# Moving seven fp32 load issues from ScalarE to SyncE, and pairing VectorE's result copies, in a batched 64x64 matmul

## Chip, cores, metric

One core of a Trainium2 chip. The metric is the device time of one execution in microseconds (us). The kernel before takes 135.17 us (median of 3 runs, 135.17 to 135.28), and its profiled execution has a span of 133.2 us.

## The reference

```python
a = randn(1024, 64, 64) fp32;  b = randn(1024, 64, 64) fp32
out = np.matmul(a, b)          # 1024 independent 64x64x64 products, fp32
```

The reference reads 33.55 MB and writes 16.78 MB.

## The kernel before

It walks 16 tiles of b and of the result (64 products each, 1 MB) and 8 tiles of a (128 products each, 2 MB). Three quarters of each a tile are loaded by GpSimd with a cast to bf16; the fourth comes as fp32 (`a_raw`) and is cast by VectorE. TensorE transposes a, VectorE spreads it into block-diagonal form (`at_bd`), TensorE multiplies, ScalarE and VectorE copy PSUM to `o_sb`, and GpSimd stores `o_sb` one tile later.

```python
A_AHEAD = 3; B_AHEAD = 4; HOLD = 2
o_v = out.rearrange("(t gh x) (mo w) n -> t (x mo) gh (w n)", gh=8, x=8, w=4)  # runs of 1 KB
# pools: a 3 buffers, b 4, work 2, o_sb 8 (1 MB each)
def load_a(s):
    ...                                       # h = 0..2: nc.gpsimd, fp32 -> bf16
    nc.scalar.dma_start(out=a_raw[...], in_=a_v[s, 3])                    # L72
def load_b(t):
    queue = nc.scalar if t % 2 else nc.sync                               # L91
    queue.dma_start(out=b_sb[:], in_=b_v[t])
def multiply(t):
    def put(lo, n):
        nc.gpsimd.dma_start(out=o_v[t, :, lo:lo+n, :], in_=o_sb[...])     # L161
    ...
    for half in range(2):
        ...                                   # 32 matmuls into o_ps, then 4 copies (L172)
        if not last:
            copies = [nc.scalar.copy] * 4
            if half:
                copies[3] = nc.vector.tensor_copy
            evacuate(o_ps, 4 * half, 4, copies)
    # stores: whole tiles; tile 14 in halves, tile 15 in quarters
...
for t in range(n_t):
    # spread and cast of t+1, load_b(t + B_AHEAD), on even t load_a(t//2 + 1 + A_AHEAD),
    # multiply(t), regroup / transpose of the next a, store(t-1)
```

## Time and profile before

| | before |
|---|---|
| time | 135.17 us (135.17 to 135.28) |
| span of the profiled run | 133.2 us |
| TensorE / VectorE / ScalarE / GpSimd busy | 51 / 72 / 65 / 27 % of the span |
| bytes at the memory | 33.55 MB read, 16.78 MB written |
| last load landed / last store issued / last store landed | 113.70 / 128.45 / 131.74 us |

Busy shares say little here: they average stages with different limits. Two views disagree about what bounds the kernel: the strip of slices shows the DMA engines full almost from end to end, and the chain that ended last is mostly compute:

```profile
DVE 29%; ACT 18%; PE 15%; DMA 13%; issue 10%; ACTq 7%; POOL 3%; SPq 1%; POOLq 1%; DVEq 0%
```

ACTq is ScalarE's own queue of issues; 7% of the chain is time in which ScalarE was held by an issue.

### The profile page before, as it was taken

What the parts mean: (1) busy time and instruction counts of PE and PEld (TensorE: products, weight loads), DVE (VectorE), ACT (ScalarE), POOL (GpSimd) and SP (SyncE); (2) the same over time, 40 slices, a digit from 0 to 9 for tenths busy, and PEclk for the clock granted to TensorE, in tenths of its full rate; (3) what the DMA queues carried; (4) which work ended last, traced back from release to release, by engine and by line L of the source; (5) the groups of instructions that cost most, each with busy time, mean ns of one, the idle gap of its engine ahead of it and who ended that gap; (6) DMA issues with size and microseconds to landing.
All of it is one profiled execution on the core that took longest, in us unless ns stands there. A gap on an engine that the chain in (4) does not pass through costs nothing.

```text
span 133.2 us, 2835 instructions
## 1 busy us (share of the span) xinstructions
PE 67.9 (51%) x1152; PEld 62.6 (47%) x1152; DVE 96.3 (72%) x121; ACT 86.8 (65%) x160; POOL 35.9 (27%) x49
## 2 busy tenths in 40 slices
PE   0000900784539259486358637951996195269300
PEld 0000900784439257475257527941995094268200
DVE  5920064943999249996999899799969996897740
ACT  3105525089950699489939992998399759969910
POOL 8981004000802017112413302030203020322460
PEclk9999995589965865579977985698569959955955
DMA  3999999999999999999999999999999999999893
GB/s 75 365 335 310 308 308 328 318 304 306 314 328 341 389 321 318 336 400 386 367 307 294 394 404 387 323 302 335 399 394 396 387 397 402 400 404 388 298 320 133
DMA packets 17485, 45.01 MB, mean 338 GB/s; under 512 B 1088, under 2 KB 1088, under 8 KB 17472
## 3 DMA queue, kind: packets, MB, share of 16 engines
q0 software_dynamic: 7440, 22.28, 54.7%
q10 hardware_dynamic: 5520, 13.11, 25.6%
q1 hardware_dynamic: 4512, 9.44, 20.1%
q8 instruction: 9, 0.15, 0.4%
q14 instruction: 4, 0.03, 0.1%
HBM read 33.55 MB, written 16.78 MB: 378 GB/s over the span
## 4 chain that ended last, share of the span: by engine, by line
DVE 29%; ACT 18%; PE 15%; DMA 13%; issue 10%; ACTq 7%; POOL 3%; SPq 1%; POOLq 1%; DVEq 0%
ACT o_sb L172 16%; DVE at_bd L128 14%; PE o_ps L184 13%; DMA b_sb<-in_b_dram 13%; DVE b_bf L139 6%; ACTq L72 4%; DVE o_sb L172 4%; POOL out_dram L161 3%; ACTq L91 3%; DVE a_bf L106 3%; PE at_ps L115 2%; DVE a_bf L103 2%; ACT b_bf L139 1%; SPq L85 1%; POOLq L274 1%
## 5 line engine op out<-in xcount | busy, mean ns | idle before, releaser
L172 ACT COPY o_sb<-o_ps 64x512 f32<-64x512 f32 x105 | 60.9, 580 | 20.3 <-PE o_ps L184 13.1
L184 PEld LDWEIGHTS <-at_bd 128*128 128x128 bf16 x1024 | 43.9, 115 | 35.5 <-DVE b_bf L139 25.1
L184 PE MATMUL o_ps<-b_bf,at_bd 128*128 128x64 bf16 x960 | 43.7, 218 | 31.2 <-DVE b_bf L139 22.4
L128 DVE COPY at_bd<-at_sb 32x1024 f32<-32x1024 f32 x64 | 45.6, 713 | 9.5 <-ACT at_sb L118 7.7
L161 POOL DMA_DIRECT2D out_dram<-o_sb x20 | 19.4, 968 | 77.9 <-DVE o_sb L172 72.5
L115 PE MATMUL at_ps<-identity,a_bf 128*128 128x128 f32 x128 | 23.3, 344 | 25.0 <-ACT a_bf L100 13.3
L115 PEld LDWEIGHTS at_ps<-identity,a_bf 128*128 128x128 f32 x128 | 19.3, 181 | 26.1 <-issue 20.8
L118 ACT COPY at_sb<-at_ps 128x512 f32<-128x512 f32 x32 | 17.4, 588 | 7.7 <-PE at_ps L115 7.3
L172 DVE COPY o_sb<-o_ps 64x512 f32<-64x512 f32 x15 | 10.4, 695 | 15.4 <-ACT o_sb L172 15.2
L139 DVE CAST b_bf<-b_sb 128x2048 bf16<-128x2048 f32 x14 | 17.4, 1245 | 0.4
L68 POOL DMA_DIRECT2D a_sb<-in_a_dram x21 | 12.5, 609 | 14.7 <-DVE a_bf L103 9.5
L106 DVE CAST a_bf<-a_raw 128x1024 bf16<-128x1024 f32 x7 | 7.0, 1003 | 1.9 <-DMA a_raw<-in_a_dram 1.9
L103 DVE COPY a_bf<-a_sb 128x3072 bf16<-128x3072 bf16 x7 | 6.7, 960 | 0.2
L100 ACT CAST a_bf<-o_sb 128x1024 bf16<-128x1024 f32 x2 | 2.0, 1042 | 7.4 <-issue 7.4
L100 DVE CAST a_bf<-o_sb 128x1024 bf16<-128x1024 f32 x2 | 2.5, 1228 | 2.6 <-DMA o_sb<-in_a_dram 2.6
L212 DVE MEMSET at_bd<- 128x4096 f32 x1 | 3.5, 3472 | 0.8 <-issue 0.8
L172 DVE COPY o_sb<-at_ps 64x256 f32<-64x256 f32 x8 | 3.4, 422 | 0.1
L139 ACT CAST b_bf<-b_sb 128x2048 bf16<-128x2048 f32 x1 | 1.9, 1898 | 2.3 <-DMA b_sb<-in_b_dram 2.3
L172 ACT COPY o_sb<-at_ps 64x256 f32<-64x256 f32 x8 | 2.9, 366 | 0.1
L209 ACT ACT_TABLE_LOAD x1 | 1.3, 1283 | 2.3 <-issue 2.3
L184 PE MATMUL at_ps<-b_bf,at_bd 128*128 128x64 bf16 x64 | 2.6, 212 | 0.3 <-DVE at_bd L128 0.3
L216 POOL MEMSET at_bd<- 128x2048 f32 x1 | 1.9, 1851 | 0.0
(12 smaller groups left out, 5.3 us busy)
## 6 DMA issues: line engine op xcount, KB each, us to landing
out_dram<-o_sb POOLq DMA_DIRECT2D x14, 1024.0 KB, 21.4
a_sb<-in_a_dram POOLq DMA_DIRECT2D x21, 256.0 KB, 19.7
a_raw<-in_a_dram ACTq DMA_DIRECT2D x7, 512.0 KB, 16.5
o_sb<-in_a_dram ACTq DMA_DIRECT2D x2, 512.0 KB, 7.3
o_sb<-in_a_dram SPq DMA_DIRECT2D x2, 512.0 KB, 6.4
out_dram<-o_sb POOLq DMA_DIRECT2D x2, 512.0 KB, 4.8
out_dram<-o_sb POOLq DMA_DIRECT2D x4, 256.0 KB, 3.7
b_sb<-in_b_dram SPq DMA_DIRECT2D x8, 0.5 KB, 16.8
```

The source lines that it names most:

```text
L68: nc.gpsimd.dma_start(out=a_sb[:, h, :, :].rearrange("p v k -> p (v k)"), in_=a_v[s, h])
L72: nc.scalar.dma_start(out=a_raw[:].rearrange("p v k -> p (v k)"), in_=a_v[s, 3])
L100: copy(a_bf[:, :, h, :], a_sb[h].rearrange("p (v k) -> p v k", v=16))
L103: nc.vector.tensor_copy(a_bf[:, :, 0:3, :], cast_sb[:].rearrange("p h v k -> p v h k"))
L106: nc.vector.tensor_copy(a_bf[:, :, 3, :], raw[:])
L115: nc.tensor.transpose(at_ps[:, vo, :], a_cols[:, 4 * vo + 2 * j + wl, :], identity[:])
L118: nc.scalar.copy(at_tiles[s][:, j, :, wl, :, :], at_ps[:].rearrange("p vo (g mp) -> p g mp vo", mp=4),)
L128: nc.vector.tensor_copy(bd[rows, :, :, :, h, :].rearrange("p j g wl mo -> p j (g wl) mo"), at_tiles[t // 2][rows, :, half, :, :, :].rearrange(
L139: (nc.vector.tensor_copy if t else nc.scalar.copy)(b_bf[:], b_sb[:])
L161: nc.gpsimd.dma_start(out=o_v[t, :, lo : lo + n, :], in_=o_sb[:, lo : lo + n].rearrange("p gh j wl n -> p (gh j wl n)"),)
L172: copies[2 * par + wl](dst, src)
L184: nc.tensor.matmul(o_ps[:, gl, g % 2, j, :], at_bd[:, j, g, :, u], b_bf[:, g, 64 * u : 64 * u + 64], start=(u == 0), stop=(u == 1),)
```

## The change

The intent is to take the slow issues of `a_raw` off ScalarE, which has copies to do, and give them to SyncE, which issues half of the b loads and does no arithmetic. VectorE's result copies, one per tile, become two on every odd tile, so that on even tiles VectorE does not wait for ScalarE. The first loads are reordered to suit SyncE's queue.

```diff
-        nc.scalar.dma_start(out=a_raw[:].rearrange("p v k -> p (v k)"), in_=a_v[s, 3])
+        nc.sync.dma_start(out=a_raw[:].rearrange("p v k -> p (v k)"), in_=a_v[s, 3])
@@ multiply
-                if half:
-                    copies[3] = nc.vector.tensor_copy
+                if half and t % 2:
+                    copies[2:] = [nc.vector.tensor_copy] * 2
@@ prologue
-        for t in range(3):
-            load_b(t)
+        load_b(0)
+        load_b(1)
         ...
         load_a(1)
+        load_b(2)
         nc.gpsimd.memset(bd_tiles[1][:, 1], 0.0)
-        for s in range(2, A_AHEAD):
-            load_a(s)
+        load_a(2)
```

## The prediction

> **What bounds the kernel now.** I read first the page's strip of forty slices and its byte counts, because the kernel does little arithmetic per byte.
>
> ```profile
> DMA  3999999999999999999999999999999999999893
> GB/s 75 365 335 310 308 308 328 318 304 306 314 328 341 389 321 318 336 400 386 367 307 294 394 404 387 323 302 335 399 394 396 387 397 402 400 404 388 298 320 133
> ...
> HBM read 33.55 MB, written 16.78 MB: 378 GB/s over the span
> ```
>
> The DMA row is full from the second slice to the last but two. The GB/s row seems to leave room (300 to 400), but a casting load counts only the bytes it writes: it reads 4 bytes for each 2 counted. The third line counts at the memory: 50.33 MB. I asked for busy time by stage next (columns after the length: busy time and count of PE, PEld, DVE, ACT and POOL, then granted clock, DMA share, GB/s).
>
> ```profile
> 0.00:10.00 10.00, 0.00 (x0) 0.00 (x0) 5.72 (x4) 1.48 (x3) 8.80 (x16) 1.00 0.80 258
> ...
> 70.00:80.00 10.00, 5.86 (x106) 5.18 (x103) 8.97 (x12) 9.79 (x19) 2.43 (x2) 0.84 1.05 364
> ...
> 110.00:120.00 10.00, 4.95 (x111) 4.50 (x110) 8.29 (x11) 8.65 (x16) 2.16 (x2) 0.81 1.03 402
> 120.00:133.00 13.00, 4.07 (x91) 3.79 (x88) 6.40 (x14) 6.75 (x15) 4.37 (x6) 0.63 0.80 287
> ```
>
> From 10 to 120 us the DMA share is above 1. No casting load is in flight after 94 us, so the 402 GB/s of 110 to 120 us is the rate at the memory. Counting each casting packet of the trace twice gives 405 GB/s for 5 to 20 us, 402 for 20 to 40, 400 for 40 to 60, and 394 to 396 from 60 to 113. The rate hardly moves while the engines go from nearly idle to busy, so I take about 400 GB/s as what the 16 DMA engines deliver here. Moving 50.33 MB at 402 takes 125.2 us of a span of 133.2.
>
> The chain of work that ended last tells another story, DVE 29% and ACT 18%, and the change is aimed at that one. The timeline shows a cause (columns: start, length, engine, line).
>
> ```profile
> 3.53 6.96 ACTq L72 DMA_DIRECT2D a_raw<-in_a_dram  x1
> ...
> 19.84 7.16 ACTq L72 DMA_DIRECT2D a_raw<-in_a_dram  x1
> ...
> 36.09 8.20 ACTq L72 DMA_DIRECT2D a_raw<-in_a_dram  x1
> ...
> 44.33 2.95 ACT L172 COPY o_sb<-o_ps 64x512 f32<-64x512 f32 x5 [5.95 <-PE at_ps L115]
> ...
> 86.69 0.69 DVE L172 COPY o_sb<-o_ps 64x512 f32<-64x512 f32 x1 [1.05 <-ACT o_sb L172]
> ```
>
> Issuing an fp32 a quarter occupies ScalarE's queue for up to 8.20 us; the copies behind it start only when it ends. The two others are 3.46 us at 53.27 and 4.22 at 65.23. Their ends (10.49, 27.00, 44.29, 56.73, 69.45) lie about half a microsecond after the landing of a transfer queued earlier on the same engine (9.99, 26.55, 43.65, 56.33, 68.97). So it is queue back-pressure: an issue that follows a b load waits until the work ahead of that b has drained.
>
> **What the Trainium skill says.** "DMA: Bandwidth & Descriptors", section "Issuing engines are not separate DMA queues", says that transfers issued by scalar, sync or gpsimd run on the same 16 DMA engines and that several issuers save only sequencer time. The trace agrees: three queues are active and their sum is pinned near 400 GB/s. "Perfetto Trace Analysis", section "Roofline", puts a single active core's practical ceiling at about 120% of 358 GB/s, about 430; the trace stays at 394 to 405, so I use the measured figure. The same page, section "DMA Instruction — HWDGE (DVE, Sync)", says the shown length of an issue includes waiting for the descriptor generator and generating; that fits issues of 0.54 to 8.20 us for equal transfers. It also calls that generator shared. The trace speaks against one engine's stalled issue holding up the other's: SyncE's b issue at 38.94 took 0.69 us inside ScalarE's 8.20 us stall. So moving the stalls to SyncE should not leave them on ScalarE.
>
> **The change part by part.** (1) Seven a-quarter issues leave ScalarE. They held its queue for 6.96 + 0.63 + 7.16 + 0.54 + 8.20 + 3.46 + 4.22 = 31.2 us, mostly while ScalarE had nothing to do. What lay on the chain: at 36.09 us. The interval between the waited-for DVE copies, 32.18, 48.49, 61.33, 73.88, 86.69, 99.51, 112.33, is 16.31 for the first pair of b tiles and 12.55 to 12.84 for the others, so that stall cost 3.5 us. At 19.84 it kept the at_sb copy until 27.05 although the first of its transposes, started at 24.15, was ready about 1 us later: 1 to 2 us. At 3.53 it kept the first a cast until 11.21, but the next things needed, b tile 0 (landed 19.81) and a quarter 1 (landed 23.28), are transfers, so nothing. Estimate for ScalarE: about 5 us off the compute chain.
>
> (2) VectorE's copies of result blocks: one per tile, 15 of 695 ns, become two on odd tiles and none on even ones, 14 in place of 15. ScalarE does 8 and 6 in place of 7 and 7. Sums hardly move. But the even tile's VectorE copy waited 1.05 us for ScalarE's third copy of the same half; that copy is now ScalarE's. Off VectorE before the even tile's a casts: 1.05 + 0.69 = 1.74 us. ScalarE's eighth copy delays its at_sb copies by 0.59: they would end near 101.15 where 100.57 was, and VectorE, ready at 100.35 in place of 102.09, would wait 0.8. The odd tile's two copies wait for the sixth ScalarE copy in place of the seventh. I make that pair 11.9 in place of 12.8: 0.9 a pair, over six steady pairs 5.4 us.
>
> (3) SyncE's order becomes b0, a1, b2, a2, a3, b4, a4, b6 and so on, with 13.1 MB on that queue and 9.4 on the other; before it was the other way round. a quarter 2 now follows b2. Before, it landed at 26.55 and b2 at 30.82. With a quarter 1 landing near 23.3, b2's 1.05 MB at about 105 GB/s to 33.3 and 0.52 MB at about 160 to 36.6, the a cast that ran at 33.78 waits until about 36.6: 2.8 us given back early in the run. Later b tiles are needed every 12 to 13 us on that queue, and a pair of b and a on it takes 10.0 + 3.3 = 13.3 us while all three queues compete, so it will be just in time.
>
> Sum for the compute chain, if data were always there: 5 + 5.4 - 2.8 = about 7.6 us earlier. It is not. b tiles landed only 3.7 to 12 us before use, odd tiles typically 5 to 6, and the faster chain eats that slack, then waits.
>
> What counts is the DMA sum. No bytes are removed. The stretches below 402 GB/s are the start and the tail. The start's is mostly first latency and first descriptors, which the change does not touch. The tail: 13 us at 402 would be 5.2 MB; at 287 it moved 3.7, so 3.7 us lie idle there. About 2 us of it are needed anyway (last store to landing, landing at 131.74, end at 133.2). So at most about 1.7 us can be won, by having stores queued when the loads run out. An earlier compute chain does this; I expect 1.2 us of it. From 135.17: 134.0.
>
> **The rivals.** First: compute is the bound, as the chain says, and the DMA row is full only because transfers wait in long queues (16 to 28 us to landing). For it: casts of b never waited for data after the start. It would give 135.17 - 7.6 = 127.6. Against it: 50.33 MB in about 125.5 us would be 401 GB/s from the first instant to the last, more than any whole run with a start and a tail can have. It could be true only if the ceiling were above 405, which no stage shows.
>
> Second: the single SyncE queue becomes the bound. Its loads stand in order, a quarter 2 and the even b tiles come late, and the final tiles stay for the end. Then the last load lands later than 113.7, fewer stores are queued behind it, and the tail of about 14 us (from last b to end in the fastest case) runs with idle DMA: 136 to 137.5. For it: 13.3 us needed against 12. Against it: while ScalarE's queue is empty SyncE's gets a larger share, and before the change ScalarE's queue carried the same 13.1 MB to 113.7.
>
> Third: VectorE's paired copies put a new wait before the next tile's matmuls, and the gain of part 2 vanishes. At a DMA bound this would change almost nothing: 134.5.
>
> **Range and chances.** The floor is about 133.5 if the rate stays at 400; a rate 1% higher, as in the first 40 us, would take another 1.2 us. So below 132.5 (2% faster) is unlikely: 0.08. The second rival in full stays under 137.9: above it 0.03. Within 2%: 0.89. Range 132.6 to 135.8.
>
> **What would show it.** Right: DMA share above 1 from 10 to 120 us as before, memory rate 395 to 405, ScalarE's queue without issues over 1 us, the long ones on SyncE, VectorE or TensorE waiting for a_raw or b_sb in mid-run, a fuller 120 to 130 us. Part 2 right: even tiles without the 1.05 us wait. Wrong: a span under 130 with a rate above 405, or holes in the DMA row before 115 us.

## The result, and the profile after

The change takes 135.87 us (median of 4 runs, 135.69 to 136.06), the kernel before beside it 135.22 (4 runs, 135.17 to 135.47). The ratio is 1.0044, interval 1.0025 to 1.0064: slower, and 0.07 us above the predicted range. Here and below a ratio is the mean time of one kernel's fast runs over that of the other's of the same rounds, so not quite the ratio of the medians quoted. A repeat on another occasion (e12, below) gave 1.0021 (1.0004 to 1.0039), so the two means put the loss at 0.3 to 0.6 us.

The page of the changed kernel: busy tenths of the DMA engines in 40 slices, GB/s, bytes at the memory, and the chain that ended last by engine.

```profile
DMA  3999999999999999999999999999999999999991
GB/s 81 371 329 310 308 317 311 305 304 297 317 304 392 354 291 322 398 385 407 320 306 341 399 392 388 305 313 358 394 387 392 393 399 403 406 382 360 333 324 49
...
HBM read 33.55 MB, written 16.78 MB: 376 GB/s over the span
...
DMA 35%; DVE 20%; ACT 13%; issue 8%; SPq 8%; PE 4%; POOL 3%; ACTq 1%; POOLq 1%; DVEq 0%
```

Three things are to be seen. The DMA row has lost the dip (8) that it had near its end. The GB/s row in the last full slices falls to 360, 333, 324 although the row above it says busy: the engines work all the time, and move less. And the chain has turned from compute (DVE and ACT 47%, ACTq 7%) into transfers (DMA 35%, SPq 8%): the change did what it was meant to do to the compute chain.

The timeline of the change shows where the stalls went (start, length, engine, line; in brackets how long the engine had waited and for what):

```profile
24.97 13.61 SPq L72 DMA_DIRECT2D a_raw<-in_a_dram  x1
...
35.36 0.69 DVE L106 CAST a_bf<-a_raw 128x1024 bf16<-128x1024 f32 x1 [7.02 <-DMA a_raw<-in_a_dram]
...
63.69 1.39 DVE L172 COPY o_sb<-o_ps 64x512 f32<-64x512 f32 x2
...
75.59 1.39 DVE L172 COPY o_sb<-o_ps 64x512 f32<-64x512 f32 x2
...
100.69 1.23 DVE L139 CAST b_bf<-b_sb 128x2048 bf16<-128x2048 f32 x1 [1.52 <-DMA b_sb<-in_b_dram]
```

SyncE is held up to 13.61 us, ScalarE's own b issues take 0.69 to 0.76. VectorE waits 7.02 us for the `a_raw` of a tile 2 ("a quarter 2" in the prediction). The paired copies come 11.9 us apart while data is there (63.69, 75.59), and the b casts begin to wait for b in the later part.

VectorE's result copies, a line of the groups of each kernel (count, then busy and mean ns of one, then idle before them and for whom):

```profile
L172 DVE COPY o_sb<-o_ps 64x512 f32<-64x512 f32 x15 | 10.4, 695 | 15.4 <-ACT o_sb L172 15.2
```

```profile
L172 DVE COPY o_sb<-o_ps 64x512 f32<-64x512 f32 x14 | 9.7, 690 | 0.3
```

Before, 15.4 us of idle time stood ahead of these copies; in the change 0.3.

The result tiles were ready earlier. The store issues at the end, from the timeline, before and then the change:

```profile
128.45 0.72 POOL L161 DMA_DIRECT2D out_dram<-o_sb  x1 [0.34 <-DVE o_sb L172]
```

```profile
122.65 2.94 POOL L161 DMA_DIRECT2D out_dram<-o_sb  x4 [0.77 <-ACT o_sb L172]
```

The last of those four issues starts at 124.88, 3.57 us before the last one of the kernel before. But what they issue lands later. Issue to landing of the halves of tile 14 (x2) and the quarters of tile 15 (x4), last column, before and then the change:

```profile
out_dram<-o_sb POOLq DMA_DIRECT2D x2, 512.0 KB, 4.8
out_dram<-o_sb POOLq DMA_DIRECT2D x4, 256.0 KB, 3.7
```

```profile
out_dram<-o_sb POOLq DMA_DIRECT2D x2, 512.0 KB, 9.1
out_dram<-o_sb POOLq DMA_DIRECT2D x4, 256.0 KB, 7.7
```

The landing of a store is when the last of its 16 DMA engines is done. Read from the landing records of the two traces (us):

| store | before | change |
|---|---|---|
| tile 9 | 115.49 | 115.47 |
| tile 10 | 118.07 | 118.06 |
| tile 11 | 120.65 | 120.64 |
| tile 12 (issued at 114.04 / 109.64) | 123.23 | 123.22 |
| tile 13 | 125.81 | 126.53 |
| tile 14, second half | 129.16 | 129.81 |
| tile 15, last quarter | 131.74 | 132.47 |

Up to tile 12 the two agree to 0.02 us, 2.58 us a tile, though the change issued tile 12 4.4 us earlier. After that the change falls behind by 0.7. The 3 MB behind tile 12 took 8.51 us before and 9.25 after; at 2.58 per MB they would have taken 7.74. The agreement to 0.02 us is partly chance: in a second profile of the change (e12, below) tiles 9 and 12 landed at 114.78 and 122.83, and the 3 MB behind tile 12 took 9.40 us. There is only one profile of the kernel before.

The stretches say why in one more way (columns: length; busy time and count of PE, PEld, DVE, ACT and POOL; granted clock; DMA share; GB/s). First the kernel before, then the change:

```profile
120.00:130.00 10.00, 4.07 (x91) 3.79 (x88) 6.40 (x14) 6.75 (x15) 4.37 (x6) 0.67 0.93 333
```

```profile
110.00:120.00 10.00, 4.88 (x89) 4.72 (x90) 9.41 (x13) 7.96 (x15) 3.04 (x3) 0.60 1.02 398
120.00:130.00 10.00, 2.31 (x44) 2.15 (x41) 3.37 (x8) 3.75 (x10) 3.59 (x5) 0.67 1.01 345
```

The idle share of the tail is gone (0.93 to 1.01), as predicted, yet the rate rose only from 333 to 345. In the change a 4096-byte store packet took 165 to 167 ns in the mean at 110 to 118 us, and 184 to 199 ns from 120 to 128. So the question for the experiments: why does a full set of DMA engines move 345 GB/s at the end, when it moved 400 before, and why does filling the tail's idle share bring nothing?

### The profile page after: what moved, and what is told of

Read it like the earlier page. It is cut to its first block, busy times and chain, and to the rows that moved or that the text cites. A ratio compares the mean times of both kernels' runs of the same rounds, so it can differ in the third digit from the quotient of the medians.

```text
span 133.9 us, 2831 instructions
## 1 busy us (share of the span) xinstructions
PE 64.7 (48%) x1152; PEld 60.0 (45%) x1152; DVE 94.3 (70%) x120; ACT 87.8 (66%) x161; POOL 37.3 (28%) x49
## 4 chain that ended last, share of the span: by engine, by line
DMA 35%; DVE 20%; ACT 13%; issue 8%; SPq 8%; PE 4%; POOL 3%; ACTq 1%; POOLq 1%; DVEq 0%
DMA a_raw<-in_a_dram 18%; DMA b_sb<-in_b_dram 17%; DVE at_bd L128 11%; ACT o_sb L172 10%; DVE b_bf L139 6%; SPq L72 5%; PE o_ps L184 4%; POOL out_dram L161 3%; ACT at_sb L118 2%; DVE o_sb L172 2%; SPq L91 2%; ACTq L91 1%; SPq L85 1%; ACT b_bf L146 1%; DVE a_bf L106 1%
## 5 line engine op out<-in xcount | busy, mean ns | idle before, releaser
L184 PEld LDWEIGHTS <-at_bd 128*128 128x128 bf16 x1024 | 42.1, 113 | 38.7 <-DVE b_bf L139 34.6
L184 PE MATMUL o_ps<-b_bf,at_bd 128*128 128x64 bf16 x960 | 40.7, 213 | 33.6 <-DVE b_bf L139 31.2
L161 POOL DMA_DIRECT2D out_dram<-o_sb x20 | 20.3, 1015 | 72.0 <-ACT o_sb L172 28.5
L115 PE MATMUL at_ps<-identity,a_bf 128*128 128x128 f32 x128 | 22.7, 337 | 23.1 <-DVE a_bf L106 11.8
L115 PEld LDWEIGHTS at_ps<-identity,a_bf 128*128 128x128 f32 x128 | 18.8, 178 | 23.5 <-issue 20.3
L68 POOL DMA_DIRECT2D a_sb<-in_a_dram x21 | 13.0, 636 | 15.6 <-DVE a_bf L103 7.4
L106 DVE CAST a_bf<-a_raw 128x1024 bf16<-128x1024 f32 x7 | 5.6, 794 | 10.4 <-DMA a_raw<-in_a_dram 10.4
L172 DVE COPY o_sb<-o_ps 64x512 f32<-64x512 f32 x14 | 9.7, 690 | 0.3
L184 PE MATMUL at_ps<-b_bf,at_bd 128*128 128x64 bf16 x64 | 3.6, 242 | 1.0 <-DVE at_bd L128 1.0
```

Source lines behind the costliest of these rows:

```text
L68: nc.gpsimd.dma_start(out=a_sb[:, h, :, :].rearrange("p v k -> p (v k)"), in_=a_v[s, h])
L106: nc.vector.tensor_copy(a_bf[:, :, 3, :], raw[:])
L115: nc.tensor.transpose(at_ps[:, vo, :], a_cols[:, 4 * vo + 2 * j + wl, :], identity[:])
L161: nc.gpsimd.dma_start(out=o_v[t, :, lo : lo + n, :], in_=o_sb[:, lo : lo + n].rearrange("p gh j wl n -> p (gh j wl n)"),)
L172: copies[2 * par + wl](dst, src)
L184: nc.tensor.matmul(o_ps[:, gl, g % 2, j, :], at_bd[:, j, g, :, u], b_bf[:, g, 64 * u : 64 * u + 64], start=(u == 0), stop=(u == 1),)
```

## The experiments

My theory after the result: the DMA engines bound both kernels; stores that have no loads beside them run slower than the mix; the faster chain finishes its loads sooner (last load landed 110.96 against 113.70) and so lengthens the slow stretch. The rivals: compute or another engine still matters; the slow packets come from the small pieces or the addresses at the end of the output; VectorE's accesses disturb the stores; or GpSimd's queue is slow.

### Each part alone

`e1_sp_only` keeps the old copies; `e2_evac_only` keeps the old loads.

```diff
 e1: load_a and the prologue as in the change; multiply as before
 e2: multiply as in the change; load_a and the prologue as before
```

> The kernel before with the a quarters on SyncE and the new load order, result copies as before. Transfer theory (the 16 DMA engines set every landing up to tile 12, the kernels differ only in the last 8 us): between 135.2 and 136.0, the store of tile 12 lands at 123.2 +/- 0.4 as in both kernels. Late-a-quarter theory (the 7.02 us wait of VectorE for a quarter 2 made the change slower): as slow as the change or slower, 135.9 to 136.5, because the wait is there and the gain of the copies is not.

> The kernel before with the new split of the result copies alone; a quarters stay on ScalarE. Transfer theory: 134.8 to 135.7, tile 12's store lands at 123.2 +/- 0.4, the last store is issued 1 to 4 us earlier than at 128.45. Late-a-quarter theory: clearly faster than before, about 0.9 us for each of six pairs less what the data withhold, 131 to 134.5.

e1: 135.47 us, ratio 1.0020 (1.0004 to 1.0035). e2: 135.72, ratio 1.0036 (1.0018 to 1.0054). Each part alone frees the compute chain: the last store was issued at 125.55 and 124.61. Each lets the loads end earlier (112.03 and 111.92), and each is a little slower than before. So neither part alone is the culprit and neither hides a gain of the other; what both have in common is the faster chain. One expectation failed: in e1 tile 12 landed at 122.51, not at 123.2 +/- 0.4 (e2: 123.14). The tail of e1:

```profile
120.00:130.00 10.00, 1.23 (x43) 1.10 (x38) 4.07 (x9) 3.92 (x10) 3.89 (x6) 0.83 1.00 347
```

Again a share of 1.00, and 347 GB/s.

### The transfers alone

`e3_transfers_alone` keeps every load and store of the change and drops the arithmetic; VectorE reads one column of each load, so that buffers still come free in the old order, and fills each `o_sb` with zeros. Its output is wrong, which doesn't matter for the time.

```diff
-            nc.vector.tensor_copy(a_bf[:, :, 3, :], raw[:])        # and all casts, transposes,
-            ...                                                    # spreads, matmuls, copies
+            nc.vector.tensor_copy(tiny[:, 3:4], raw[:, 0, 0:1])    # one column of each load
```

> Wrong result on purpose (zeros): all loads and stores of the changed kernel, in its order and queues, with one tiny read of each loaded tile and a fill of each result tile in place of the arithmetic. Transfer theory: 132.5 to 135.5, memory rate 394 to 406 GB/s between 10 and 115 us, so the whole arithmetic costs at most 3 us. Compute theory (chain of DVE, ACT and PE is the bound): well under 130.

135.25 us, ratio 1.0007 (0.9986 to 1.0027). A kernel with the transfers of the change and no arithmetic takes the same time: the transfers bound the change. For the kernel before, which moves the same bytes in the same time but issues them from other queues, this is inferred. With these transfers in this order, faster compute can bring nothing that these runs could resolve. Its stretches (only DVE, ACT and POOL have busy columns here):

```profile
110.00:120.00 10.00, 5.46 (x5) 0.00 (x0) 4.70 (x7) 1.00 1.02 392
120.00:130.00 10.00, 0.00 (x0) 0.00 (x0) 0.53 (x1) 1.00 0.97 332
```

All its stores were issued by 119.81, so nothing waits for compute in the second line, and still 332 GB/s. VectorE does nothing then, so it isn't VectorE that slows the stores.

### More work for VectorE

```diff
+            nc.vector.memset(junk[:], 0.0)      # e4: the change, plus a 128x512 fill per tile
```

> The changed kernel with one more fill of 128x512 fp32 on VectorE per tile (about 0.45 us, 16 of them, about 7 us in all; VectorE is the busiest engine). Transfer theory: 135.3 to 137, the extra work goes into waits for data and the tail. Compute theory: 141 to 143.

135.63 us, ratio 1.0030 (1.0014 to 1.0046), between the change's two measurements (1.0021 and 1.0044). The 16 added fills took 7.8 us of VectorE and cost nothing that can be seen, where a compute bound was expected to give 141 to 143: the chain of compute is not the bound.

### Stores with no loads at all

`e5_stores_alone` has only the stores of such zero tiles, `e10` issues them from SyncE and ScalarE in place of GpSimd, `e9` writes them in runs of 8 KB instead of 1 KB (the layout of the result is wrong). Their outputs are wrong, which doesn't matter for the times.

```diff
 e5:  e3 without the loads
 e10: e5, stores issued by nc.sync and nc.scalar in turn
 e9:  e5 with
-    o_v = out.rearrange("(t gh x) (mo w) n -> t (x mo) gh (w n)", gh=8, x=8, w=4)
+    o_v = out.rearrange("(t p2) (h r) n -> t (p2 h) (r n)", p2=64, h=2)...   # 8 KB runs
```

> Wrong result on purpose (zeros): the 16 result stores alone, same pieces and same queue, no loads. In the five traces so far the 4096-byte store packets take 165 ns until 6 to 8 us after the last load has landed, then more and more of them 185 to 250. Write-only theory (the memory takes about 7 us of stores without loads at 400 GB/s and then less): packets 165 ns for the first 7 us or so, then 185 to 250, about 330 to 350 GB/s for the rest. Address or end-of-run theory (the last tiles' addresses or small pieces are slow): 165 ns for the first 11 tiles, slow only in the last four.

> Wrong result on purpose (zeros): the stores alone, issued by SyncE and ScalarE in turn instead of GpSimd. If the slow store-only rate comes with GpSimd's queue: near 400 GB/s. If it lies in writing 1 KB runs to memory without reads beside it: 330 GB/s or less, as with GpSimd (328).

> Wrong result on purpose (zeros): the stores alone from GpSimd, but each partition writes 8 KB in one run instead of eight runs of 1 KB. If the short runs make store-only slow: near 400 GB/s, packets near 165 ns. If any store-only stretch is slow: 320 to 340 GB/s as with 1 KB runs.

60.96, 56.68 and 50.59 us. The GB/s rows of the three pages (40 slices of spans of 59.2, 54.9 and 48.8 us), e5, e10, e9:

```profile
GB/s 0 0 0 232 343 304 324 318 316 318 327 316 321 335 316 332 332 335 321 327 332 324 332 327 329 327 329 329 329 329 324 338 332 327 338 346 263 208 158 0
```

```profile
GB/s 0 0 26 351 326 351 330 341 338 323 346 330 320 351 327 322 354 329 350 329 350 325 350 329 349 350 330 349 339 339 348 342 348 343 347 342 345 345 307 0
```

```profile
GB/s 0 0 0 141 396 423 409 349 423 409 430 369 430 403 409 423 403 416 396 423 383 423 409 403 423 396 416 389 423 383 409 369 379 406 406 399 383 255 40 0
```

Stores in 1 KB runs with no loads beside them move about 326 GB/s from the first moment (6 to 50 us), about 339 from another pair of queues (5 to 50 us), and about 403 in 8 KB runs (6 to 42 us). So the rate of the tail, 345, is near that of stores alone in short runs, and stores from another pair of queues were little faster. The length of the runs makes the difference: e9 also changed the packets from 4096 to 8192 bytes, but e15 and e16 below keep 4096 and are fast as well. Something else did change with the queues: in e5 the 16 engines ended the stores further and further apart, up to 4.61 us, and in e10 0.29 to 0.63. The packets of e10 were also smaller (1024 bytes), so which of the two did it is not known. In e5 VectorE was done with its fills by 35.1 us, and the stores went on at 330 GB/s, which rules VectorE out a second time. One thing does not fit: stores alone are slow from the start, whereas in the full kernels the store packets keep 165 ns for some 6 to 8 us after the last load. Why there is such a grace stays open.

### Loads kept beside the last stores

`e8` adds four b loads to the change at the end, so that loads run beside the last stores (correct result, one look).

```diff
-            if t + B_AHEAD < n_t:
-                load_b(t + B_AHEAD)
+            load_b(t + B_AHEAD if t + B_AHEAD < n_t else t)
```

> The changed kernel with four more loads of b tiles (already used ones, into free b buffers, never read) in the slots of tiles 12 to 15, so that loads go on to the end; 4.19 MB more, right result. Write-only theory: store packets of the tiles 11 to 13 stay at 165 to 172 ns while the extra loads run; the sum of rates stays at 390 to 405; total about 10.5 us longer than the change, or less (4.19 MB at 400 GB/s, less what the tail wins). Address or end-of-run theory: the store packets of tile 12 on take 185 to 250 all the same, with loads beside them.

145.84 us, some 10 more for 4 MB more. The stretches of its last part:

```profile
110.00:120.00 10.00, 0.00 (x0) 0.10 (x1) 3.94 (x5) 0.25 (x2) 0.89 (x1) 0.62 1.03 395
120.00:130.00 10.00, 5.80 (x103) 5.51 (x103) 5.35 (x9) 9.73 (x20) 3.05 (x3) 0.50 1.03 393
130.00:138.00 8.00, 1.52 (x29) 1.36 (x26) 3.23 (x8) 2.13 (x6) 3.05 (x5) 0.50 1.03 393
```

393 GB/s up to 138 us; the last load landed at 140.69, the last store at 142.53. The same pieces of the same tiles went to the same addresses with packets of 169 to 173 ns in the mean of each 2 us from 110 to 138. So the small pieces and the addresses are refuted as the cause: what counts is whether loads run beside the stores.

### Loads that end later

If a long stretch of stores alone is what costs, the change with later loads should lose its handicap. `e7` is the change, `e11` the kernel before, each with b loaded three tiles ahead rather than four (and three buffers for b).

```diff
-    B_AHEAD = 4
+    B_AHEAD = 3
...
-        load_b(3)
```

> The changed kernel with b loads three tiles ahead instead of four (and three b buffers). Write-only theory: loads end later, nearer to their use; if the compute chain keeps up, 133.5 to 135.5; if b tiles come too late the tail after the last load (about 14 us) sets the end, 135.5 to 138. Rival (DMA bytes alone set the time): 135.7 to 136.1 as the change.

> The kernel before with b loads three tiles ahead instead of four (three b buffers), nothing else. Write-only theory (what differs between these kernels is how long stores run without loads): last load lands after 113.7 us, and the time is 134.6 to 135.2 if the compute chain keeps up; this chain is slower than the changed one, so it may also lose: above 135.5 only if the last load lands so late that less than about 14 us remain. Bytes-only rival: 135.0 to 135.3 as before.

e7: 134.93 us, ratio 0.9991 (0.9968 to 1.0013). Its last load landed at 116.77, the slow packets begin only at about 124, and the last store landed at 131.58 where the change had 132.47:

```profile
120.00:130.00 10.00, 2.54 (x50) 2.42 (x47) 3.38 (x8) 5.60 (x13) 4.35 (x6) 0.67 0.99 372
```

372 GB/s in place of 345, at the same share. No handicap is left to be seen, though the interval overlaps that of the change's repeat (1.0004 to 1.0039); a gain over the kernel before is not shown, as the interval includes 1.

e11: 145.48 us, ratio 1.0771 (1.0733 to 1.081), far from the expected 134.6 to 135.2. I read its trace as bound by the compute chain, for the a issues of ScalarE now follow a b issue directly; its last load landed only at 127.85. From its timeline and its waits (total, times, longest):

```profile
58.96 5.51 ACTq L72 DMA_DIRECT2D a_raw<-in_a_dram  x1
```

```profile
DVE o_sb L172 <- ACT o_sb L172: 25.8, 8, 7.1
```

The two together show that what the change does on the chain is real, and large: with three tiles ahead it is worth 145.48 - 134.93 = 10.55 us. With four, the kernel before has enough slack to hide its stalls behind the transfers, and the gain has nowhere to go.

### Some stores through SyncE

```diff
-            nc.gpsimd.dma_start(
+            (nc.sync if t % 4 == 1 else nc.gpsimd).dma_start(      # e6: the kernel before
```

> The kernel before with the stores of tiles 1, 5, 9 and 13 issued by SyncE instead of GpSimd: a second queue with stores gives them a larger share, so fewer stores are left when the loads end. Write-only theory: loads end later than 113.7 us, the stretch of stores without loads is shorter than 18.0 us, and the time is 133 to 134.8. If only bytes over 400 GB/s matter: 134.8 to 135.6.

140.70 us, ratio 1.0402 (1.0376 to 1.0428): a miss. The store of tile 1, issued on SyncE at 39.83, landed at 74.13; the b load behind it, issued at 55.10, landed at 84.73; the last load landed at 119.57. On SyncE's queue the stores also went out in packets of 1024 bytes, not 4096. It tells nothing of the tail. The loads behind a store on SyncE came late; whether their place behind it or the small packets is the reason was not tested.

### The change again

> The changed kernel itself once more, beside the others on one chip: 135.7 to 136.1, last load at 111 us +/- 1, ratio to before 1.003 to 1.006.

135.51 us, ratio 1.0021 (1.0004 to 1.0039), last load 110.41, last landing 132.23. No edit. The loss is smaller than expected (135.7 to 136.1, ratio 1.003 to 1.006), but real: both intervals lie above 1.

### Both kernels with a fast tail

If only the slow stores ate the predicted 1.2 us, both kernels with long runs should differ by it. `e13` (change) and `e14` (before) write 8 KB runs, `e15` and `e16` write 4 KB runs (two halves per tile). All four write a wrong layout; all bytes are written.

```diff
-    o_v = out.rearrange("(t gh x) (mo w) n -> t (x mo) gh (w n)", gh=8, x=8, w=4)
+    o_v = out.rearrange("(t p2) (h r) n -> t (p2 h) (r n)", p2=64, h=2).rearrange("t p (gh f) -> t p gh f", gh=8)
@@ put: out=o_v[...] as one run (cut here)
@@ e15, e16 only
-            whole = t < n_t - 2
+            whole = False
```

> Wrong result on purpose (each partition's 8 KB of a result tile go to one run of memory, so elements land elsewhere): the changed kernel with long store runs. If the failed step of the prediction is the rate of the store-only tail: the last stores run near 400 GB/s, packets near 165 ns to the end, last landing 130.5 to 131.3 in place of 131.8 to 132.5, time 134.0 to 134.8, that is 0.7 to 1.7 us under the change. If the tail is slow for another reason: 135.4 to 135.9 as the change.

> Wrong result on purpose, the kernel before with the same long store runs. Its tail waits for the last tile's arithmetic (last store issued at 128.45), so long runs should help it less: 134.6 to 135.2, and slower than the changed kernel with long runs by 0.3 to 1.2 us: the gain that the prediction had expected. If the changed kernel with long runs is no faster than this one, the rate of the tail is not what took the gain.

143.73 us (ratio 1.0633, 1.0607 to 1.066) and 138.19 (1.0241, 1.0214 to 1.0269). Inconclusive for the tail, since the edit changed something else. The GB/s row of e13:

```profile
GB/s 77 397 318 305 306 325 307 305 293 314 310 373 355 294 343 411 388 316 316 375 403 366 320 314 408 419 406 416 363 394 379 356 214 300 293 2 268 320 302 6
```

There are holes from slice 33 on: the store packets had become 8192 bytes, the loads came last (117.94 and 119.96 us), and the kernels waited for them. The Trainium skill says in "DMA: Bandwidth & Descriptors", section "Queues, rings and completion order", that a DMA engine goes round its queues a packet at a time; larger store packets then take a larger share from the loads, which agrees with the later last loads. Hence the pair with 4 KB runs:

> Wrong result on purpose: the changed kernel with results in 4 KB runs of memory, each tile stored in two halves, so that store packets keep the 4096 bytes that they have in the change (with 8 KB runs they became 8192 and the stores took the loads' turns). Loads should then end at 109 to 113 us as in the change. If the store-only rate took the gain: last stores near 400 GB/s, packets 160 to 172 ns to the end, time 133.8 to 135.0. If not: 135.4 to 136.

> Wrong result on purpose: the kernel before with the same 4 KB runs in halves. Loads end at 112 to 115 us; its last stores wait for the last tile's arithmetic: 134.5 to 135.3, slower than the changed kernel with 4 KB runs by 0.3 to 1.2 us if the store-only rate is what took the gain.

e15, the change: 134.94 us, ratio 0.9992 (0.9974 to 1.0009). e16, before: 134.76, ratio 0.9977 (0.9958 to 0.9996). Their stretches, e15 then e16:

```profile
110.00:120.00 10.00, 7.19 (x128) 6.88 (x128) 8.51 (x15) 8.21 (x16) 4.48 (x7) 0.54 1.03 417
120.00:130.00 10.00, 0.00 (x0) 0.00 (x0) 1.55 (x4) 1.54 (x5) 2.17 (x4) 0.50 0.81 329
```

```profile
110.00:120.00 10.00, 5.91 (x120) 5.63 (x120) 8.79 (x13) 8.87 (x16) 2.75 (x5) 0.68 1.02 415
120.00:130.00 10.00, 1.54 (x45) 1.42 (x42) 4.07 (x9) 4.17 (x11) 3.00 (x6) 0.67 0.81 327
```

The fast tail is there: 415 to 417 GB/s, the 4096-byte packets took 159 to 163 ns in the mean to the end, and the last stores land at 130.24 and 130.01, some 2 us earlier. But my expectation that the change would now win 0.3 to 1.2 us failed: its advantage over the kernel before is nil, or slightly negative. So the low rate of the tail alone does not explain the missing gain. The pair does not show that no gain was to be had either, for e16 is not the old chain with a fast tail: its last load landed at 111.38 (before: 113.70) and its last store was issued at 125.80 (before: 128.45), so the late stores that the change was to cure came earlier in it too. (The time fell by less than the landings, 0.3 to 0.9 us, since GpSimd's last wait ended 2.3 us after the last landing instead of 0.66. These kernels issue more stores, but e13 and e14 waited 1.7 us with the old number; the reason was not tested.)

## Why the prediction was wrong

- **The bound (right).** DMA, not compute. e3 has no arithmetic and the same time as the kernel before, e4 has more and lies between the two measurements of the change. The first rival (127.6 us) is refuted, and the rate in mid-run, recounted in stretches of 10 us with casting packets taken twice, stayed at 393 to 406 (in the kernel before at 393 to 404, where the prediction reads 394 to 405).
- **The stalls (right).** They moved to SyncE (up to 13.61 us) and left nothing on ScalarE.
- **Part 2 (right).** The even tile's wait is gone and the steady pair takes 11.66 to 11.94 us, where 11.9 was predicted; from 75.59 on, 12.20 to 13.44.
- **The late a quarter 2 (right in kind, too large).** It landed at 35.34, predicted 36.6; the cast came 1.6 us later than before, predicted 2.8.
- **The faster chain then waits for data (right).** The slack that it gives as 3.7 to 12 us recounts as 5.3 to 12.0, from landing to cast. In the change b casts waited 1.01 and 1.52 us at 87 and 100 us, and the whole tail came 3.57 us earlier by issue. The second rival, that SyncE's queue makes the last load late, is refuted: it came 2.7 us earlier.
- **A fuller tail (right), and what it brings (wrong).** The step that failed is the last sum: "at most about 1.7 us can be won, by having stores queued when the loads run out ... I expect 1.2 us of it". The stores were queued, the share rose from 0.93 to 1.01, and the last landing came 0.73 us later, not 1.2 us earlier. Two terms of that sum were wrong.
  - *The idle share was taken for idle time on the path.* It is a mean over 16 engines, and a store is complete when the slowest has done its part. On the path of the landings the kernel before lost 8.51 - 7.74 = 0.77 us behind tile 12, not 1.7: that is all that a fuller tail could win at the rate of tiles 9 to 12. And the change did win in the mean: its 16 engines finished the last quarter at 131.17 on average, before at 131.57. But they finished it 2.87 us apart, before 0.37, and the last one came at 132.47, before at 131.74. In e15 and e16 it is the same: on average 128.36 and 128.63, the last 130.24 and 130.01. Before, the spread shrank from 2.43 us at tile 12; I read this as fast engines waiting for stores while the slow ones caught up, so that filling the tail gave work to engines that had been idle without harm. No experiment shows this reading, and none varied the drift alone in a full kernel.
  - *The tail was reckoned at 402 GB/s.* Stores alone in 1 KB runs move about 326 to 339 (e5, e10), and the tail of the change, at a full share, moved 345. The prediction's own sum with 345 for 402 is 13 us at 345 = 4.49 MB, less 3.73 moved, 0.76 MB or 2.2 us, less the 2 us that it holds needed: an estimate of 0.2 us to be won, not 1.7. (The 2 us is loose too: the last store took 3.29 us from issue to landing, and the span ended 1.45 us after that.) Because the change ends its loads sooner, the stretch from last load to last landing grew from 18.0 to 21.5 us.

That the change became slower, and not only no faster, agrees with a longer stretch of stores alone, but is not explained by it alone, as e15 and e16 show. The kernels stand roughly in the order of their last load:

| kernel | last load landed | to last landing | ratio |
|---|---|---|---|
| change, loads 3 ahead (e7) | 116.77 | 14.8 us | 0.9991 |
| before | 113.70 | 18.0 | 1 |
| e1 | 112.03 | 19.9 | 1.0020 |
| e2 | 111.92 | 20.6 | 1.0036 |
| e4 | 111.11 | 21.3 | 1.0030 |
| change | 110.96 | 21.5 | 1.0044 (repeat 1.0021) |
| e3, no arithmetic | 109.96 | 22.1 | 1.0007 |

e3 breaks the order, so the relation is not a law. That loads beside the stores keep these fast is shown by e8, and e7 agrees; that the end of the loads sets the sign is argued. Open as well: why stores keep their 165 ns for 6 to 8 us after the last load, and why the engines drift apart by 2 to 3 us. The stores of e10, issued by SyncE and ScalarE, drifted by no more than 0.63 us; the last stores of the change on those queues were not tried. "Perfetto Trace Analysis", section "Identifying the Most-Contended Engine", warns that with 16 DMA engines occupancy misleads and says to use the utilization of the memory; the trace agrees, as the share went up by 0.08 and the end came later.

No version clearly beats both. e7 is 0.4 to 0.7% under the two medians of the change (135.51 and 135.87, measured in other rounds) and not distinguishable from the kernel before; e16 is 0.2% faster but writes another layout.

## What to carry to other kernels

When a kernel without its arithmetic takes the same time (e3: ratio 1.0007), work on bytes, run lengths and on which transfers run side by side, not on waits of the compute engines, however long the chain of waits makes them look. Before counting idle DMA share at the end as time to be won, look at the engine that ends last, and at the rate that stores reach with no loads beside them. A faster compute chain also pulls loads forward; finishing the loads early is not always a gain. Here prefetching three tiles ahead in place of four took the change from 135.51 or 135.87 to 134.93 us, but the kernel before from 135.07 to 145.48, where issues then stalled ScalarE (e11).

## What the Trainium skill lacked or had wrong

- "DMA: Bandwidth & Descriptors", section "Specifications", gives 512 bytes as the least transfer for line rate. Here stores alone in 1 KB runs moved about 326 to 339 GB/s (e5, e10) and in 8 KB runs about 403 (e9); the same 1 KB runs beside loads took part in 390 to 400. That the mix of reads and writes matters is missing.
- The same page: nothing gives the size of the stall when an issue follows a large load on one queue. Here a 512 KB issue held its engine up to 13.61 us (change) and 8.20 (before).
- "Perfetto Trace Analysis", section "Roofline": its ceiling of about 430 GB/s for one core was not reached in any stretch of 10 us of any run: at most 408 with 1 KB runs (e11) and 417 with 4 KB runs (e15) or 8 KB runs (e13).
- "DMA: Bandwidth & Descriptors", section "Latency and other measured facts", names two DMA engines that usually lag, but no page has the size of the drift between the first and last of the 16 engines that finish one store, or says that a mean share hides it: 0.37 us (before) and 2.87 us (change) for the last quarter, up to 4.61 in e5 with stores from GpSimd, up to 0.63 in e10 with stores from SyncE and ScalarE. Which engines lagged the records of these runs do not tell.
- No page has the time of GpSimd's last wait after the last landing: 0.66 us in both kernels, 2.3 us in e15 and e16 (34 stores), 1.7 us in e13 and e14 (20 stores, as in both kernels); the cause was not tested.
